# Sums, differences and weight splits placed on VectorE alone, in a two-layer diffusion backbone

## The chip, the core and the metric

The kernel runs on one NeuronCore of a Trainium2 chip. TensorE (PE in the profile, with its weight loads as PEld) multiplies, VectorE (DVE), ScalarE (ACT) and GpSimd (POOL) work on tiles in SBUF, SyncE (SP) issues the DMAs that bring the weights from HBM. TensorE writes to PSUM, which has 8 banks of 128 partitions x 512 floats. Each engine works through its own instructions in order; semaphores hold an instruction until what it needs is done. The metric is the time on the device in microseconds, the median of three runs.

## The reference

All data is float32. There are 512 latent tokens and 256 context tokens with 1024 features, and two layers. Cut to what matters:

```
for l in range(2):
    ml, mc = ada(c, ada_w[l], ada_b[l]), ada(c_ctx, ada_w[l], ada_b[l])     # 9 vectors of 1024 each
    h += 0.5 * m[2] * swiglu(modulate(h, norm_ffn1, m[0], m[1]), ffn1_w_gu, ffn1_w_down)
    n  = modulate(h, norm_mix, m[3], m[4])
    h += m[5] * concat(retention(n @ w_in), fourier(..), attention(..), spatial_gate(..)) @ w_out
    h += 0.5 * m[8] * swiglu(modulate(h, norm_ffn2, m[6], m[7]), ffn2_w_gu, ffn2_w_down)
out = rms_norm(h_lat)
# swiglu(h) = (silu(a) * b) @ w_down, with a, b = split(h @ w_gu); w_gu 1024 x 5632, w_down 2816 x 1024
```

In the second layer the context is needed only up to the keys and values of the mixing; its second feed-forward block then runs on the 512 latent tokens.

## The kernel before

**Numbers in two parts.** TensorE multiplies float32 data in a rounded format (fp32r). To keep accuracy each operand is split: ScalarE casts it (`hi`), and a subtraction makes the rest, `lo = x - hi`. A product is three matmuls: hi hi, hi lo, lo hi (`mm3`). So every piece of weights, 128x512, needs a cast on ScalarE and a subtraction (`w_subs`), and so does every tile of activations (`split_t`). A *split* below is that subtraction.

**Fewer products.** Most of the three first feed-forward blocks is multiplied by quarters in a scheme with 7 products in place of 8 (Strassen's, in a form with sums T1 to T4 of activation quarters and in-place sums of weight quarters). The sums of weight quarters are made by GpSimd in place in the raw weight tiles (`w_sums`, `raw<-raw`); those of activations by `t_task` and `hid_sums`.

**A feed-forward block** takes its 22 columns of 128 hidden features in segments of 4 (the first of 2 or 6). For each segment: two `pair`s (7 products x 2 weight pieces, each piece 12 matmuls of 128x384), giving hidden tiles; then the *down stage*, `down_fast`, again 7 products x 2 pieces:

```
for no, nm, bank, start, end, to in ((1, "11", "b", ...), (5, "T1", "c", ...), (6, "T2", "b", ...),
                                     (3, "22", "c", ...), (7, "T3", "b", ...), (2, "21", "a", ...), (4, "T4", "b", ...)):
    for dh in range(2):
        w = yield from self.getp(("dw", l, which, f, no, dh))
```

After every half piece (6 matmuls, one bank) VectorE adds the bank, times the gate, into the residual H (`upd`, `H<-b,modG,H`): a tile of 384 tokens in one instruction, or, where it crosses from latent to context tokens, a 128 and a 256 one, here called an update pair. A down stage has 28 such half pieces: 4 of 384, 16 pairs, 8 of 384.

**Weights** come as raw tiles of 512 KB (4 buffers), are cut in 2 to 4 pieces, and up to 8 pieces (`NP`) are held ready or in use. A raw tile is given back, and the next one loaded, when its last piece is split.

**The order of the instructions** is made by a planner in the program itself: tasks are generators with priorities, and a clock for each engine (`Eng`: a fixed cost and a rate, for VectorE 68 ns and 0.96 elements/ns, for GpSimd 100 ns and 0.42) says when it would be free. The planner decides when a task emits its next instruction, and twice it decides on which engine: `any2` (a sum, difference or product of two SBUF tiles goes to whichever of VectorE and GpSimd would end first), and `w_subs` (a weight split goes to GpSimd when it is at least `FAR` = 3 pieces ahead of TensorE, VectorE's clock is ahead of the planner's time and GpSimd's is not). Its clocks know nothing of engines getting in each other's way. In the profile all instructions that go through `Eng` have line 127; TensorE's have lines 242 to 283.

Of the kernel before, what the change touches and what calls it, by code (L numbers as in the profile page):

```python
# [35 lines left out]
def f32v(ap):  # L36
    return ap.bitcast(F32)


def _free(ap):  # L40
    n = 1
    for x in ap.shape[1:]:
        n *= x
    return n
# [94 lines left out]


class Kernel:
    FAR, SB, NS = 3, 130.0, 3
    RP = 2
    TG, BM = 300.0, 4000.0
    NM, NK = 3, 0
# [72 lines left out]

    def any2(self, op, out, a, b):

        n = _free(out)
        if any(x.tensor.name == self.psn for x in (a, b)):
            return self.V(op, out, a, b)
        v = max(self.V.t, self.t) + self.V.fixed + n / self.V.rate
        g = max(self.G.t, self.t) + self.G.fixed + n / self.G.rate
        return (self.V if v <= g else self.G)(op, out, a, b)


    def pe(self, cols, rows, floor, reads, out):
# [213 lines left out]
    def w_subs(self):  # L443
        for j, (key, r, view, dep, free) in enumerate(self.pieces):
            yield (lambda: j in self.wh)
            w, hi, src = self.wh.pop(j)
            far = (lambda: j - self.pnext >= self.FAR and self.G.t <= self.t)
            yield (lambda: (self.force > j or self.V.t <= self.t + self.slack(j, self.SWV) or far()) and self.T.ready(hi) <= self.t + 200.0)
            lo = w[:, 1]
            if len(src.shape) == 3:  # L450
                lo = lo.rearrange("p (a b) -> p a b", a=src.shape[1])
            (self.G if far() and self.V.t > self.t else self.V)("tensor_sub", lo, src, f32v(hi))
            self.wt[j] = w
            self.pcv = j + 1
            if free:
                self.dead(self.rawt.pop(r))
                self.rlive -= 1
                self.w_load()
# [1833 lines left out]
```

## Time and profile before

| | |
|---|---|
| median of 3 runs | 2625.94 us (2621.76 to 2627.26) |
| profiled execution | 2626.68 us, its span 2624.7 us |
| TensorE busy | 2539.7 us, 97%, mean granted clock 0.989 |
| VectorE busy | 2029.7 us, 77% |
| ScalarE busy | 1252.0 us, 48% |
| GpSimd busy | 1318.5 us, 50% |
| HBM read | 247.59 MB, 95 GB/s over the span |

TensorE's matmuls are pipelined, so its busy time is no proof of full speed; where it waits is told better by the chain of waits, which follows the work that ended last back to the start. A row of the timeline may stand for several instructions in a row (xN); its names are those of the first ones' form. Names are `out<-in`: H the residual, b a PSUM bank, w a weight piece, raw a raw weight tile, u and t activations.

### The profile page before, as it was taken

The numbers are of one execution on the slowest core, as the hardware profiler recorded it, in microseconds if no ns is written. First come the engines' busy times: TensorE is split into PE (matmuls) and PEld (weight loads), VectorE is DVE, ScalarE is ACT, GpSimd is POOL, SyncE is SP. The second block draws the span as 40 slices with busy tenths as digits, with TensorE's granted clock in tenths as the row PEclk, the third lists the DMA queues.
The fourth block names the chain that finished last, engine by engine and source line by source line (L and its number), as shares of the span: only waits on it lengthen the run. The fifth ranks groups of instructions, "written<-read, shape, count | busy, mean of one in ns | idle before, by whom it ended". The sixth has DMA issues, their size and how long they took to land.

```text
span 2624.7 us, 44882 instructions
## 1 busy us (share of the span) xinstructions
PE 2539.7 (97%) x17116; PEld 2422.2 (92%) x17116; DVE 2029.7 (77%) x3526; ACT 1252.0 (48%) x2576; POOL 1318.5 (50%) x1080
## 2 busy tenths in 40 slices
PE   7999999999999989999999999999999999899998
PEld 5888999999998978889999989999999888899998
DVE  5766787878679886776787877878878788987776
ACT  4433344455646543333444544444446645544445
POOL 3635656733232354555774547667734331544443
PEclk9999999999999999999999999999999999999999
DMA  8455322222111155553223112222232211133332
GB/s 283 142 187 177 113 73 89 65 83 57 49 57 41 43 173 183 188 169 129 81 65 97 49 42 77 68 72 73 73 91 65 61 57 41 57 101 101 100 103 72
DMA packets 193622, 252.57 MB, mean 96 GB/s; under 512 B 12188, under 2 KB 160896, under 8 KB 193408
## 3 DMA queue, kind: packets, MB, share of 16 engines
q1 hardware_dynamic: 187152, 246.82, 29.6%
q10 hardware_dynamic: 6256, 2.90, 0.4%
q8 instruction: 134, 2.20, 0.4%
q14 instruction: 80, 0.66, 0.1%
HBM read 247.59 MB, written 2.10 MB: 95 GB/s over the span
## 4 chain that ended last, share of the span: by engine, by line
PE 76%; DVE 16%; DMA 2%; issue 2%; ACT 2%; POOL 1%; SPq 0%; ACTq 0%; POOLq 0%; DVEq 0%
PE b L242 47%; PE b L244 25%; DVE u L127 7%; DVE t L127 3%; DVE w L127 3%; PE b L255 2%; PE b L283 2%; DVE H L127 1%; DMA adaraw<-in_ada_w_dram 1%; ACT u L127 1%; ACT w L127 1%; DMA raw<-in_ffn_w_gu_dram 1%; SPq L393 0%; POOL nacc L127 0%; ACT t L127 0%
## 5 line engine op out<-in xcount | busy, mean ns | idle before, releaser
L242 PE MATMUL b<-u,w 128*128 128x384 f32 (+1 forms) x8736 | 1449.1, 326 | 9.9 <-DVE adasum L127 5.4
L242 PEld LDWEIGHTS b<-u,w 128*128 128x128 f32 x8736 | 1429.0, 189 | 28.2 <-issue 15.3
L127 ACT CAST w<-raw 128x512 fp32r<-128x512 f32 x949 | 575.7, 620 | 564.3 <-PE b L242 216.2
L127 DVE TENSOR_TENSOR w<-raw,w 128x512 fp32r<-128x512 f32 x674 | 640.9, 962 | 228.6 <-ACT w L127 220.4
L127 POOL TENSOR_TENSOR raw<-raw 128x512 f32<-128x512 f32 x416 | 616.1, 1502 | 345.1 <-DMA raw<-in_ffn_w_gu_dram 130.0
L127 POOL TENSOR_TENSOR w<-raw,w 128x512 fp32r<-128x512 f32 x275 | 383.6, 1408 | 509.3 <-ACT w L127 468.9
L244 PE MATMUL b<-u,w 128*128 128x256 f32 (+2 forms) x3888 | 582.4, 308 | 15.4 <-ACT u L127 11.5
L244 PEld LDWEIGHTS b<-u,w 128*128 128x128 f32 x3888 | 541.9, 193 | 39.7 <-ACT u L127 13.1
L127 DVE SCALAR_TENSOR_TENSOR H<-b,modG,H 128x128 f32<-128x128 f32 (+3 forms) x832 | 365.1, 474 | 134.6 <-PE b L244 76.6
L244 PE MATMUL b<-w,u 128*128 128x256 f32 x2172 | 281.1, 286 | 1.8 <-DVE w L127 1.8
L244 PEld LDWEIGHTS b<-w,u 128*128 128x128 f32 x2172 | 271.1, 193 | 6.8 <-DVE w L127 2.2
L127 ACT CAST u<-u 128x384 fp32r<-128x384 f32 (+4 forms) x318 | 140.9, 464 | 126.6 <-DVE u L127 83.2
L127 DVE TENSOR_TENSOR u<-u 128x384 fp32r<-128x384 f32 (+8 forms) x226 | 164.2, 746 | 11.5 <-ACT u L127 10.7
L127 POOL TENSOR_TENSOR u<-u 128x384 fp32r<-128x384 f32 (+3 forms) x138 | 119.9, 878 | 95.0 <-ACT u L127 94.5
L127 ACT CAST u<-t 128x384 fp32r<-128x384 f32 (+2 forms) x162 | 74.5, 471 | 185.8 <-DVE t L127 182.2
L127 ACT COPY t<-b 128x384 f32<-128x384 f32 (+5 forms) x223 | 99.6, 448 | 125.0 <-PE b L242 79.3
L127 POOL TENSOR_TENSOR nacc<-nacc,t 128x256 f32<-128x256 f32 (+2 forms) x112 | 89.7, 801 | 123.2 <-ACT t L127 119.1
L127 DVE TENSOR_TENSOR t<-t,b 128x384 f32<-128x384 f32 (+3 forms) x216 | 106.1, 494 | 32.9 <-PE b L242 31.9
L127 DVE TENSOR_TENSOR u<-t,u 128x384 fp32r<-128x384 f32 (+2 forms) x150 | 104.8, 704 | 10.9 <-ACT u L127 9.8
L127 DVE TENSOR_TENSOR u<-u,t 128x384 f32<-128x384 f32 (+1 forms) x108 | 102.6, 958 | 12.6 <-POOL u L127 4.8
L244 PE MATMUL b<-u 128*128 128x256 f32 (+5 forms) x516 | 104.6, 336 | 3.0 <-DVE u L127 2.8
L127 DVE TENSOR_TENSOR u<-b,u 64x256 fp32r<-64x256 f32 (+3 forms) x175 | 91.1, 525 | 20.3 <-ACT u L127 18.4
(99 smaller groups left out, 1556.9 us busy)
## 6 DMA issues: line engine op xcount, KB each, us to landing
raw<-in_ffn_w_gu_dram SPq DMA_DIRECT2D x176, 512.0 KB
adaraw<-in_ada_w_dram SPq DMA_DIRECT2D x114, 512.0 KB
raw<-in_ffn_w_down_dram SPq DMA_DIRECT2D x88, 512.0 KB
raw<-in_w_in_dram SPq DMA_DIRECT2D x28, 512.0 KB
raw<-in_w_out_dram SPq DMA_DIRECT2D x32, 256.0 KB
u<-in_ada_w_dram SPq DMA_DIRECT2D x14, 512.0 KB
u<-in_ada_w_dram SPq DMA_DIRECT2D x16, 384.0 KB
raw<-in_w_in_dram SPq DMA_DIRECT2D x16, 256.0 KB
```

The lines of the kernel that those rows point to most:

```text
L127: getattr(self.eng, name)(*args, **kw)
L242: self.nc.tensor.matmul(out, a, b, start=start, stop=stop, skip_group_check=True)
L244: self.nc.tensor.matmul(out, a, b, start=start, stop=stop)
L255: self.nc.tensor.matmul(out[q:q + 32], self.cs[:, k], x, start=start, stop=stop)
L283: self.nc.tensor.transpose(out, in_, self.ident[:p, :p])
```

## The change

`any2` no longer chooses: every sum, difference or product that goes through it is issued on VectorE. In `w_subs` the third condition and the choice of engine go: a weight split is always VectorE's, issued when the piece is due or when VectorE's clock is near the planner's time. GpSimd keeps the sums of weight quarters, most of the sums for the norms (`nacc`), the power for 1/sqrt and the decay tables. The constant `FAR` goes.

```
-    FAR, SB, NS = 3, 130.0, 3
+    SB, NS = 130.0, 3
...
     def any2(self, op, out, a, b):
-        n = _free(out)
-        if any(x.tensor.name == self.psn for x in (a, b)):
-            return self.V(op, out, a, b)
-        v = max(self.V.t, self.t) + self.V.fixed + n / self.V.rate
-        g = max(self.G.t, self.t) + self.G.fixed + n / self.G.rate
-        return (self.V if v <= g else self.G)(op, out, a, b)
+        return self.V(op, out, a, b)
...
             w, hi, src = self.wh.pop(j)
-            far = (lambda: j - self.pnext >= self.FAR and self.G.t <= self.t)
-            yield (lambda: (self.force > j or self.V.t <= self.t + self.slack(j, self.SWV) or far()) and self.T.ready(hi) <= self.t + 200.0)
+            yield (lambda: (self.force > j or self.V.t <= self.t + self.slack(j, self.SWV)) and self.T.ready(hi) <= self.t + 200.0)
...
-            (self.G if far() and self.V.t > self.t else self.V)("tensor_sub", lo, src, f32v(hi))
+            self.V("tensor_sub", lo, src, f32v(hi))
```

In the programs' order, 453 instructions leave GpSimd for VectorE: 275 weight splits (128x512) and 178 others, mostly splits of 128x384 (59) and 128x256 (53) activations. With VectorE's clock later, the planner also gives 26 additions of the norm's shift to ScalarE that VectorE had.

Where it shows most is the down stage. The rows are those of the third one in the second layer's first block; `w_17262` is the eighth of its 14 pieces, `w_17272` the ninth, `u_17305`/`u_17301` and `u_17340`/`u_17334` hold the sums of hidden tiles for the sixth and seventh product. On GpSimd before:

```order
L127 TENSOR_TENSOR w_17262<-raw_17042,w_17262 128x512
L127 TENSOR_TENSOR w_17272<-raw_17014,w_17272 128x512
L127 TENSOR_TENSOR raw_17042<-raw_17111,raw_17042 128x2x256
L127 TENSOR_TENSOR u_17292<-u_16716,u_17292 128x384
L127 TENSOR_TENSOR u_17305<-u_16981,u_17305 128x384 x2
L127 TENSOR_TENSOR u_17340<-u_16981,u_17340 128x384 x2
L127 TENSOR_TENSOR w_17323<-raw_17042,w_17323 128x512
L127 TENSOR_TENSOR w_17338<-raw_17092,w_17338 128x512
```

and on VectorE before, at the same place, where no weight split stands between the 28 half pieces' updates:

```order
L127 TENSOR_TENSOR u_17292<-u_16716,u_17292 128x384
L127 SCALAR_TENSOR_TENSOR H_91<-b_78,modG_14952,H_91 128x128
L127 SCALAR_TENSOR_TENSOR H_91<-b_78,modG_14952,H_91 128x256
L127 SCALAR_TENSOR_TENSOR H_91<-b_78,modG_14952,H_91 128x128
L127 SCALAR_TENSOR_TENSOR H_91<-b_78,modG_14952,H_91 128x256
L127 SCALAR_TENSOR_TENSOR H_91<-b_78,modG_14952,H_91 128x128
L127 SCALAR_TENSOR_TENSOR H_91<-b_78,modG_14952,H_91 128x256
L127 TENSOR_TENSOR u_16981<-u_16981,t_17030 128x384
```

With the change, VectorE from the last split of activations on:

```order
L127 TENSOR_TENSOR u_17334<-u_16981,u_17334 128x384 x2
L127 SCALAR_TENSOR_TENSOR H_91<-b_78,modG_14949,H_91 128x128
L127 SCALAR_TENSOR_TENSOR H_91<-b_78,modG_14949,H_91 128x256
L127 SCALAR_TENSOR_TENSOR H_91<-b_78,modG_14949,H_91 128x128
L127 SCALAR_TENSOR_TENSOR H_91<-b_78,modG_14949,H_91 128x256
L127 TENSOR_TENSOR w_17262<-raw_17042,w_17262 128x512
L127 SCALAR_TENSOR_TENSOR H_91<-b_78,modG_14949,H_91 128x128
L127 SCALAR_TENSOR_TENSOR H_91<-b_78,modG_14949,H_91 128x256
L127 TENSOR_TENSOR w_17272<-raw_17018,w_17272 128x512
L127 TENSOR_TENSOR w_17332<-raw_17042,w_17332 128x512
```

The split of the eighth piece has moved from GpSimd's list to a place in VectorE's that lies behind the updates of the stage's first 14 half pieces (4 of 384 and 10 pairs, two of the pairs in the rows shown) and behind all its activation splits. Nine further weight splits follow among the later updates. Counted through the program, the same sequence stands in eight of the twelve down stages of this kind: the last two of each block of the first layer, and all four of the second layer's first block.

## Rows read from the trace of the kernel before

**Rows 1.** Page, part 1: busy time, share of the span, instructions.

```profile
PE 2539.7 (97%) x17116; PEld 2422.2 (92%) x17116; DVE 2029.7 (77%) x3526; ACT 1252.0 (48%) x2576; POOL 1318.5 (50%) x1080
```

**Rows 2.** Page, part 4: the chain of waits by engine, share of span.

```profile
PE 76%; DVE 16%; DMA 2%; issue 2%; ACT 2%; POOL 1%; SPq 0%; ACTq 0%; POOLq 0%; DVEq 0%
```

**Rows 3.** Chain of waits, 1537 to 1945 us, by engine, tile, line.

```profile
by line: PE b L242 99.9%; PE b L244 0.1%
```

**Rows 4.** Chain of waits, 560 to 975 us, same columns.

```profile
by line: PE b L244 59.9%; DVE u L127 13.5%; DVE t L127 5.8%; PE b L283 4.8%; DVE w L127 3.7%; issue 2.8%; DVE H L127 2.4%; ACT u L127 2.2%; DMA adaraw<-in_ada_w_dram 1.2%; DVE sm L127 1.0%; ACT t L127 0.7%; ACT w L127 0.5%; POOL u L127 0.4%
```

**Rows 5.** Stretches of the span: length, busy time of each engine, clock.

```profile
core 0: us, PE busy (x) PEld busy (x) DVE busy (x) ACT busy (x) POOL busy (x), PEclk, DMA share, GB/s
...
300.00:560.00 260.00, 260.00 (x1503) 260.00 (x1503) 205.35 (x310) 115.24 (x224) 166.74 (x123) 1.00 0.26 80
...
560.00:975.00 415.00, 400.32 (x2951) 374.13 (x2950) 343.61 (x728) 235.75 (x512) 151.18 (x159) 0.99 0.20 63
...
1222.00:1440.00 218.00, 218.00 (x1264) 218.00 (x1263) 171.85 (x255) 99.57 (x195) 137.39 (x97) 1.00 0.25 76
...
1537.00:1945.00 408.00, 408.00 (x2357) 408.00 (x2357) 322.00 (x477) 183.37 (x359) 264.93 (x190) 1.00 0.25 77
```

**Rows 6.** Groups by line and form: count, busy us, mean ns, idle before.

```profile
L127 DVE TENSOR_TENSOR w<-raw,w 128x512 fp32r<-128x512 f32 x674 | 640.9, 962 | 228.6 <-ACT w L127 220.4 <-PE b L242 0.3
...
L127 POOL TENSOR_TENSOR w<-raw,w 128x512 fp32r<-128x512 f32 x275 | 383.6, 1408 | 509.3 <-ACT w L127 468.9 <-PE b L244 24.6 <-DMA raw<-in_ffn_w_down_dram 14.1
...
L127 POOL TENSOR_TENSOR raw<-raw 128x512 f32<-128x512 f32 x416 | 616.1, 1502 | 345.1 <-DMA raw<-in_ffn_w_gu_dram 130.0 <-DVE w L127 102.9 <-DMA raw<-in_ffn_w_down_dram 56.8
...
L127 POOL TENSOR_TENSOR u<-u 128x384 fp32r<-128x384 f32 x59 | 62.3, 1071 | 24.4 <-ACT u L127 24.4
```

**Rows 7.** VectorE in order of time: start us, length us, instruction, waits.

```profile
1724.28 1.88 DVE L127 TENSOR_TENSOR w<-raw,w 128x512 fp32r<-128x512 f32 x3
...
1746.89 1.03 DVE L127 TENSOR_TENSOR u<-u 128x384 fp32r<-128x384 f32 x2 [0.58 <-ACT u L127]
...
1769.36 1.78 DVE L127 TENSOR_TENSOR w<-raw,w 128x512 fp32r<-128x512 f32 x1
```

**Rows 8.** GpSimd in order of time, before and in one down stage.

```profile
1762.58 1.60 POOL L127 TENSOR_TENSOR w<-raw,w 128x512 fp32r<-128x512 f32 x1
...
1768.98 1.61 POOL L127 TENSOR_TENSOR raw<-raw 128x512 f32<-128x512 f32 x1
...
1773.95 3.01 POOL L127 TENSOR_TENSOR w<-raw,w 128x512 fp32r<-128x512 f32 x2 [3.37 <-ACT w L127]
...
1785.12 8.80 POOL L127 TENSOR_TENSOR w<-raw,w 128x512 fp32r<-128x512 f32 x7
```

**Rows 9.** VectorE in order of time, the same down stage.

```profile
1774.46 0.61 DVE L127 SCALAR_TENSOR_TENSOR H<-b,modG,H 128x384 f32<-128x384 f32 x1
...
1774.99 0.54 DVE L127 TENSOR_TENSOR u<-u,b 128x384 f32<-128x384 f32 x1
...
1775.45 2.31 DVE L127 SCALAR_TENSOR_TENSOR H<-b,modG,H 128x384 f32<-128x384 f32 x5
...
1777.68 0.94 DVE L127 TENSOR_TENSOR u<-u 128x384 fp32r<-128x384 f32 x1
...
1778.55 2.03 DVE L127 SCALAR_TENSOR_TENSOR H<-b,modG,H 128x128 f32<-128x128 f32 x6
...
1781.18 1.83 DVE L127 TENSOR_TENSOR u<-u,t 128x384 f32<-128x384 f32 x2 [0.60 <-POOL u L127]
...
1782.93 7.38 DVE L127 SCALAR_TENSOR_TENSOR H<-b,modG,H 128x128 f32<-128x128 f32 x22
...
1790.61 0.74 DVE L127 SCALAR_TENSOR_TENSOR H<-b,modG,H 128x128 f32<-128x128 f32 x2 [0.30 <-PE b L242]
```

**Rows 10.** VectorE, unbroken updates in the first such down stage.

```profile
395.51 6.58 DVE L127 SCALAR_TENSOR_TENSOR H<-b,modG,H 128x128 f32<-128x128 f32 x20
```

**Rows 11.** VectorE's waits, 1537 to 1945 us: total, times, longest.

```profile
DVE w L127 <- ACT w L127: 49.9, 48, 2.3
```

## Prediction

> **What bounds the kernel now.** I read the busy times first, then the chain of waits, then stretches, then single stages. TensorE is busy 97% of the span, VectorE 77%, GpSimd 50% [rows 1], and the chain is 76% TensorE and 16% VectorE [rows 2]: 0.16 x 2624.7 = 420 us in which something waits for VectorE. These are not spread evenly. From 1537 to 1945 us the chain is TensorE alone [rows 3]. The same holds where TensorE is busy all of a stretch [rows 5]: 300 to 560, 1222 to 1440, 1537 to 1945, together 260 + 218 + 408 = 886 us. These are the feed-forward blocks once the modulation is computed; nothing that VectorE or GpSimd does there costs time now, at the granted clock of 1.00. In the mixing, 560 to 975, TensorE has 60 + 5 of 100 and VectorE most of the rest [rows 4].
>
> So the change can win only outside the 886 us, and can lose everywhere. The first question is whether TensorE still never waits inside them.
>
> **The prices.** Three weight splits in a row with GpSimd idle take 1.88 us, 0.60 each after the first's start-up [rows 7]; the mean over all of VectorE's is 962 ns and GpSimd's mean is 1408 [rows 6]. Beside one of GpSimd's sums, of 1.61 from 1768.98, a split took 1.78 [rows 7, 8]. Two splits of 384 take 1.03, so 0.47 each and 0.08 for the end [rows 7]; on GpSimd one is 1071 ns [rows 6]. An update pair is 7.38 / 11 = 0.67; five updates (three of 384 and a pair) take 2.31, so a 384 one is (2.31 - 0.67 - 0.08) / 3 = 0.52 [rows 9].
>
> **What VectorE gains in work.** 275 weight splits x 0.60 = 165 us, and 178 others at 0.47 or below, at most 84: some 230 us in all. Off go 26 shift additions, a few us, and the time that VectorE's own instructions now lose beside the moved ones. VectorE goes from 2029.7 to some 2200 us, 84% of the span. The average would fit. The down stages do not.
>
> **One down stage, step by step.** A piece is 12 matmuls at 408.00 / 2357 = 0.173 us [rows 5], 2.08 us; a half piece 1.04. At 1790.61 VectorE waits for TensorE again [rows 9], with the 16th pair, which is the update of the 20th half piece (4 of 384 precede the pairs). So the stage began on TensorE at 1790.55 - 20 x 1.04 = 1769.75, and its eighth piece at 1769.75 + 7 x 2.08 = 1784.3. VectorE begins the first update at 1774.46 [rows 9], 3.7 us after that half piece ended at 1770.8: it comes into the stage late, from splits that met GpSimd's sums, and works off the lag until 1790. It can, because GpSimd has the splits: two from 1773.95 (the eighth and ninth piece's) and seven from 1785.12 [rows 8].
>
> With the change VectorE's list from the first update to the eighth piece's split holds 4 updates of 384 (2.08), an addition from PSUM (0.47, since it took 0.54 [rows 9]), 10 pairs (6.70), 8 instructions of 384 on SBUF tiles (3.76; before it was three) and the split (0.60): 13.6 us. From 1774.46 that ends at 1788.1. TensorE wants the piece at 1784.3, so it waits 3.8 us. The wait is not only a lag: the split is queued behind the update of the 14th half piece, which TensorE finishes just as it reaches the eighth piece. Even a VectorE with no lag makes it wait 0.67 + 0.60 = 1.27 us, and again 0.67 + 0.60 - 1.04 = 0.23 at the ninth piece, whose split stands behind the 15th half piece. That is the lower end, 1.5 us.
>
> When VectorE starts the stage is the unknown. Ahead of it one split joins its list (+0.60), and the GpSimd split of 1.60 at 1762.58 [rows 8] goes, which can free VectorE of up to that much waiting, less if it waited for a weight sum instead. Net -1.0 to +0.6; I take -0.4, near the middle. Within the 13.6 us I add no contention: GpSimd's one remaining sum of these tiles needs the eighth split done first. If I am wrong on that, 8 instructions lose 0.94 - 0.55 = 0.39 each (the u<-u at 1777.68 against the first of two free ones) [rows 7, 9] and the split 1.18: 4.3 us more. So a stage costs 3.4 us, with ends at 1.5 and 3.8 + 0.6 + 4.3 = 8.7.
>
> Behind the waiting piece nothing else gets late at first: the nine splits that follow are 0.60 each, with updates of 0.67 or 2 x 0.52 between them, under 2.08 a piece. They give raw tiles back some 12 us later than GpSimd did, so the next block's weights land later; the next pair's first piece is needed only at 1769.75 + 14 x 2.08 = 1798.9 plus the wait, and I cost that at nothing. If it is late too, the stage goes towards its upper end.
>
> Eight stages have this sequence of instructions, and unbroken runs of 20 or 22 updates in the trace show the same saturated VectorE, in the first of them at 395.51 as in the one above [rows 9, 10]. 8 x 3.4 = 27 us. In the other four, TensorE also has the modulation's matmuls in between and waits for their DMAs; I take 0 there (ends 0 and 4 x 1.5 = 6).
>
> **The rest of the span**, 2624.7 - 886 = 1739 us, has VectorE on the chain for 420 of them, 24%. Spread evenly, 230 x 1739 / 2624.7 = 152 us of new work lie there; if a quarter is felt, +37. Against it, a weight split loses (962 - 680) / 962 = 29% of its time beside GpSimd (a free one lasts 1.88 - 2 x 0.60 = 0.68) [rows 6, 7]; of GpSimd's time the moved splits and those of 384 alone are (383.6 + 62.3) / 1318.5, a third [rows 1, 6]. At most 420 x 0.29 x 0.34 = 41 us leave the chain; half of it, since much of VectorE's chain reads PSUM, is 20. GpSimd itself has 1% of the chain [rows 2], 26 us, of which perhaps half goes. +37 - 20 - 13 = +4, which I round to 0, with ends -67 (41 + 26, nothing added) and +37.
>
> **The sum** is made on the profiled execution: 2626.68 (span 2624.7 and 2 us around it) + 27 + 0 = 2653.7; the median of the runs shown is 0.7 lower, so 2653.
>
> **Rivals.**
> *The port is freed and the kernel gets faster.* Mechanism: splits on VectorE wait for GpSimd's at the layer's seams and in the mixing, and with 453 of these gone the chain shortens there by the 41 + 26 us that are the upper end above, less half of the +37. For it: 962 against 680 ns, and the two subtractions at 1781.18 that waited 0.60 for GpSimd's split and then took 1.83, not 1.03 [rows 7, 9]. Against it: GpSimd keeps its 616.1 us of weight sums [rows 6], and TensorE must not wait in the down stages, where the order makes it. With no stall there: 2626 - 67 + 18 = 2577 at best, with the middle value of relief 2626 - 33 + 18 = 2611. It decides if VectorE enters the stages without lag and the seams give more than 12 us. The Trainium skill, page "SBUF — State Buffer", section "Who interferes with whom", speaks for this rival: VectorE and GpSimd share a pair of ports as an exclusive lock, and a VectorE instruction with two SBUF inputs fully blocks against a GpSimd one that reads SBUF. The trace agrees with it: 1.78 us for a split beside a sum, 0.60 without [rows 7, 8].
> *The lead hides it.* Eight piece buffers are 8 x 2.08 = 16.6 us of matmuls, and VectorE's splits often wait for ScalarE's casts, 48 times and 49.9 us from 1537 to 1945 [rows 11]: there the weights are as far ahead as the buffers let them. If such lead carried through the stage, nothing would change: 2626 (2621 to 2631). Against it: the instructions are issued in order, and the split stands behind the update.
> *VectorE becomes the bound.* If sums meet the splits after all, or raw tiles come late, the stage costs its upper end, and other stages start to wait: 2626 + 8 x 8 = 2690.
>
> **Chances.** A stall in the eight stages of 1.5 to 5.5 us with the rest within +-10: 2632 to 2672, 0.70. Port freed and faster: 0.11. Lead hides it: 0.09. VectorE the bound, above 2672: 0.10. What a measurement can tell from no change is about 0.2%, 5 us. So faster 0.11, same 0.10 (the second rival and a little of the forecast's lower edge), slower 0.79. The range must leave out 2 in 10: it reaches from 2622 to 2678.
>
> **What would show it.** In the changed profile: TensorE's waits on VectorE's w, none now from 1537 to 1945, come to about 3.4 us a stage, once per 87 us, and the stretch of 408 grows by 14; VectorE at 84%, GpSimd at 770 us or so; VectorE's mean split nearer 800 ns than 962. It is wrong if the chain from 1537 to 1945 is still TensorE alone, or if the stall sits elsewhere: at the seams, or at the first piece after a down stage.

## The result, and the profile after

The kernel after takes **2640.29 us** (median of 4 runs, 2637.9 to 2642.16) against 2623.85 us of the kernel before on the same chip: a ratio of 1.0059, 95% interval 1.0047 to 1.007. It is slower, by 0.6%. Forecast were 2653 us and a range of 2622 to 2678.

The page of the kernel after, its busy times and the chain by engine, beside [rows 1, 2]:

```profile
PE 2548.8 (97%) x17116; PEld 2430.1 (92%) x17116; DVE 2157.0 (82%) x3954; ACT 1259.1 (48%) x2601; POOL 795.5 (30%) x627
...
PE 74%; DVE 20%; DMA 2%; issue 2%; ACT 1%; POOL 0%; SPq 0%; POOLq 0%; DVEq 0%; ACTq 0%
```

VectorE has 428 instructions more, but only 127 us more busy time, where some 170 were forecast. The chain from 1537 to 1945 us, which was TensorE alone [rows 3], is now (TensorE's lines 242 and 244 are 237 and 239 in the kernel after):

```profile
by line: PE b L237 72.5%; DVE u L127 9.0%; DVE H L127 7.7%; DVE w L127 6.5%; DVE t L127 3.0%; issue 1.0%; ACT w L127 0.3%; DVEq L127 0.0%; ACTq L127 0.0%
```

TensorE's waits from 1530 to 2000 us (total us, times, longest) are one row:

```profile
PE b L237 <- DVE w L127: 15.4, 4, 4.2
```

With two each from 300 to 600 (7.4 us) and 1240 to 1500 (7.4 us) that makes eight waits, 30.2 us, 3.8 us each. The stage of [rows 8, 9] in order of time, TensorE and VectorE, from the first update to the eighth piece:

```profile
1780.64 0.60 DVE L127 SCALAR_TENSOR_TENSOR H<-b,modG,H 128x384 f32<-128x384 f32 x1
...
1786.75 1.01 DVE L127 TENSOR_TENSOR u<-u 128x384 fp32r<-128x384 f32 x2
1787.68 1.01 DVE L127 TENSOR_TENSOR u<-u,t 128x384 f32<-128x384 f32 x2
1788.62 2.68 DVE L127 SCALAR_TENSOR_TENSOR H<-b,modG,H 128x128 f32<-128x128 f32 x8
1791.22 1.01 DVE L127 TENSOR_TENSOR u<-u 128x384 fp32r<-128x384 f32 x2
1792.16 1.37 DVE L127 SCALAR_TENSOR_TENSOR H<-b,modG,H 128x128 f32<-128x128 f32 x4
1793.46 0.67 DVE L127 TENSOR_TENSOR w<-raw,w 128x512 fp32r<-128x512 f32 x1
...
1794.19 21.13 PE L237 MATMUL b<-u,w 128*128 128x384 f32 x105 [3.71 <-DVE w L127]
```

The list was forecast at 13.6 us and took 13.49 (1780.64 to 1794.13). But the stage loses more than its wait. These are stretches around the wait in the same stage (columns as in [rows 5]; in brackets the number of instructions, the number ahead of the DMA share is the granted clock):

```profile
1785.00:1790.40 5.40, 5.40 (x32) 5.15 (x30) 5.40 (x16) 4.42 (x9) 0.00 (x0) 1.00 0.00 0
1790.40:1794.20 3.80, 0.09 (x2) 0.01 (x1) 3.73 (x10) 0.00 (x0) 0.00 (x0) 0.87 0.00 0
...
1796.00:1798.00 2.00, 2.00 (x8) 2.00 (x7) 2.00 (x5) 0.00 (x0) 0.00 (x0) 0.50 0.00 0
1798.00:1800.00 2.00, 2.00 (x8) 2.00 (x7) 0.82 (x4) 0.00 (x0) 0.00 (x0) 0.50 0.73 186
1800.00:1802.00 2.00, 2.00 (x13) 2.00 (x13) 2.00 (x6) 0.62 (x1) 0.00 (x0) 1.00 0.96 335
```

TensorE stands for 3.7 us, and the clock falls from 1.00 to 0.50, the 1.2 GHz level, until about 1800: 6 matmuls begin in 2 us instead of 12 (the counts in the rows take in those that reach over an edge), while the busy time says 2.00 of 2.00. This is one of the two longer falls, 6.8 us from 1793.2; in the other six stages the clock stood at 0.50 for 3.4 us, as in the stage at 1608:

```profile
1608.90:1612.30 3.40, 3.40 (x12) 3.40 (x12) 2.18 (x5) 0.00 (x0) 0.00 (x0) 0.50 0.00 0
1612.30:1615.00 2.70, 2.70 (x18) 2.70 (x17) 2.22 (x7) 0.00 (x0) 0.00 (x0) 1.00 0.78 223
```

If one takes the k-th weight matmul of either trace and follows the difference of their times, the stretches with the eight stages lose 12.3 us (two stages, 390 to 500 us of the kernel before), 11.2 (two, 1250 to 1430) and 23.9 us (four, 1590 to 1940), together **47.3 us, 5.9 a stage**: 3.8 of waiting and 2.1 behind it. The clock accounts for nearly all of these 2.1: behind the eight waits it stood at 0.50 for 31.6 us in all, and half of that, 15.8 us, is 2.0 a stage. All the rest of the span gives **34.0 us** back; 47.3 - 34.0 = 13.3 us, and the spans differ by 13.6.

Where these 34 come from shows best at the seam of the two layers. The kernel before, GpSimd, VectorE and TensorE in order of time:

```profile
1505.84 1.62 POOL L127 TENSOR_TENSOR raw<-raw 128x512 f32<-128x512 f32 x1
1506.22 3.21 DVE L127 TENSOR_TENSOR u<-t,u 128x384 fp32r<-128x384 f32 x2
1507.41 3.17 POOL L127 TENSOR_TENSOR w<-raw,w 128x512 fp32r<-128x512 f32 x2
...
1510.54 4.73 POOL L127 TENSOR_TENSOR raw<-raw 128x512 f32<-128x512 f32 x3
...
1512.47 3.20 DVE L127 TENSOR_TENSOR t<-u 128x384 f32<-128x384 f32 x2
1515.78 0.56 DVE L127 TENSOR_TENSOR u<-u,t 128x384 f32<-128x384 f32 x1
...
1520.62 0.69 PE L244 MATMUL b<-u,w 128*128 128x384 f32 x1 [5.22 <-ACT u L127]
```

Beside GpSimd a sum of 384 takes 1.6 us, and 0.56 as soon as GpSimd stops at 1515.3; TensorE waits 5.22 us for what comes of them. In the kernel after GpSimd stands idle until 1508.5, and TensorE goes through:

```profile
1502.82 28.76 PE L239 MATMUL b<-u,w 128*128 128x384 f32 x165
...
1505.14 0.55 DVE L127 TENSOR_TENSOR u<-u 128x384 f32<-128x384 f32 x1
1505.61 0.55 DVE L127 TENSOR_TENSOR u<-t,u 128x384 fp32r<-128x384 f32 x1
1506.08 1.01 DVE L127 TENSOR_TENSOR t<-u 128x384 f32<-128x384 f32 x2
```

This seam gives 9.5 of the 34 us back; the others are spread over the span and were not traced one by one. Sums of this kind over the whole span, and the splits [rows 6], in the kernel after:

```profile
L127 DVE TENSOR_TENSOR w<-raw,w 128x512 fp32r<-128x512 f32 x949 | 848.5, 909 | 196.2 <-ACT w L127 186.8 <-PE b L237 2.2
...
L127 DVE TENSOR_TENSOR u<-u 128x384 fp32r<-128x384 f32 x152 | 78.0, 547 | 3.1 <-ACT u L127 3.1
```

The 93 of the kernel before took 655 ns each. The splits' mean fell only from 962 to 909: matched in time with GpSimd's instructions, 605 of the 949 ran alone at 685 ns, but 155 lay wholly beside one at 1439. The Trainium skill, page "SBUF — State Buffer", section "Who interferes with whom", has VectorE and GpSimd contend for a shared port pair, an exclusive lock, when the VectorE instruction reads two SBUF tiles and the GpSimd one reads SBUF, and not when the VectorE instruction reads one. The trace agrees, down to the sums with an operand in PSUM (t<-t,b of 384): in the kernel before they took 551 ns alone and 548 wholly beside a GpSimd instruction.

### The profile page after: what moved, and what is told of

The parts are those of the page before. It is cut to its first block, busy times and chain, and to the rows that moved or that the text cites. A ratio compares the mean times of both kernels' runs of the same rounds, so it can differ in the third digit from the quotient of the medians.

```text
span 2638.3 us, 44737 instructions
## 1 busy us (share of the span) xinstructions
PE 2548.8 (97%) x17116; PEld 2430.1 (92%) x17116; DVE 2157.0 (82%) x3954; ACT 1259.1 (48%) x2601; POOL 795.5 (30%) x627
## 4 chain that ended last, share of the span: by engine, by line
PE 74%; DVE 20%; DMA 2%; issue 2%; ACT 1%; POOL 0%; SPq 0%; POOLq 0%; DVEq 0%; ACTq 0%
PE b L237 42%; PE b L239 29%; DVE u L127 8%; DVE w L127 5%; DVE H L127 4%; DVE t L127 3%; PE b L250 2%; PE b L278 2%; DMA adaraw<-in_ada_w_dram 2%; ACT u L127 1%; ACT w L127 0%; DMA u<-in_x_dram 0%; DVE sm L127 0%; DMA raw<-in_ffn_w_down_dram 0%; DMA raw<-in_ffn_w_gu_dram 0%
## 5 line engine op out<-in xcount | busy, mean ns | idle before, releaser
L237 PE MATMUL b<-u,w 128*128 128x384 f32 (+1 forms) x8736 | 1465.2, 328 | 38.0 <-DVE w L127 31.8
L127 DVE TENSOR_TENSOR w<-raw,w 128x512 fp32r<-128x512 f32 x949 | 848.5, 909 | 196.2 <-ACT w L127 186.8
L127 POOL TENSOR_TENSOR raw<-raw 128x512 f32<-128x512 f32 x416 | 629.5, 1533 | 1110.6 <-DMA raw<-in_ffn_w_gu_dram 657.9
L127 DVE TENSOR_TENSOR u<-u 128x384 fp32r<-128x384 f32 (+7 forms) x364 | 191.2, 549 | 6.8 <-ACT u L127 5.8
L127 POOL TENSOR_TENSOR nacc<-nacc,t 128x256 f32<-128x256 f32 x102 | 80.9, 793 | 359.3 <-ACT t L127 357.8
L127 POOL TENSOR_TENSOR rs<-mse,mhalf 128x2 f32<-128x2 f32 (+4 forms) x41 | 43.8, 1071 | 231.0 <-DVE mse L127 220.9
L127 DVE TENSOR_TENSOR u<-t,u 128x384 fp32r<-128x384 f32 (+3 forms) x167 | 101.4, 610 | 3.2 <-ACT u L127 2.6
L127 ACT CAST u<-b 64x256 fp32r<-64x256 f32 (+3 forms) x175 | 78.1, 453 | 40.1 <-PE b L278 37.3
L239 PEld LDWEIGHTS b<-u 128*128 128x128 f32 (+1 forms) x516 | 79.1, 183 | 16.3 <-DVE u L127 5.1
```

The lines of the kernel that those rows point to most:

```text
L127: getattr(self.eng, name)(*args, **kw)
L237: self.nc.tensor.matmul(out, a, b, start=start, stop=stop, skip_group_check=True)
L239: self.nc.tensor.matmul(out, a, b, start=start, stop=stop)
```

## The experiments

The times are medians; "stages" is what the eight down stages cost against the kernel before in TensorE's matmuls, and "rest" the remainder up to the last weight matmul, from one trace each. The stretches are those given above; with e2 and e5 some 1.3 and 4 us of "stages" lie in them behind the eight stages. The kernel before, measured beside each group of these runs, had medians of 2624.8 to 2626.1 us, against 2623.85 beside the kernel after; so 2 us between two rows say nothing.

| kernel | us | ratio to before, 95% | stages | rest |
|---|---|---|---|---|
| after (both parts) | 2640.3 | 1.0047 to 1.007 | +47.3 | -34.0 |
| e1 sums alone | 2645.2 | 1.0057 to 1.0085 | +25.1 | -8.3 |
| e2 splits alone | 2631.7 | 1.0009 to 1.0027 | +8.8 | -4.5 |
| e3 after, down splits on GpSimd | 2610.3 | 0.9929 to 0.9955 | +14.7 | -29.5 |
| e4 after, 17 fillers | 2668.0 | 1.0144 to 1.0174 | +71.3 | -30.6 |
| e5 after, lead 2 | 2621.9 | 0.998 to 0.9998 | +16.9 | -26.2 |
| e6 after, lead 4 | **2588.9** | 0.9849 to 0.9876 | +3.8 | -41.6 |
| e7 after, 16 fillers | 2639.5 | 1.004 to 1.0068 | +44.9 | -29.4 |
| e8 before, down splits alone on GpSimd | 2606.9 | 0.992 to 0.9945 | 0.0 | -16.5 |
| e9 after, 30 fillers | 2632.1 | 1.0015 to 1.0035 | +35.5 | -29.7 |
| e10 before, lead 4 | 2627.2 | 0.9997 to 1.0015 | +1.8 | -2.5 |
| e11 after, lead 6 | 2601.8 | 0.9897 to 0.9921 | +7.0 | -35.2 |
| e12 splits alone, lead 4 | 2609.5 | 0.9926 to 0.995 | 0.0 | -14.7 |

**The two parts apart.** e1 is the kernel before with the sums' part of the change:

```
 def any2(self, op, out, a, b):
-    ...
+    return self.V(op, out, a, b)
```

> Half of the change: sums and differences of activations go to VectorE, weight splits keep the choice between VectorE and GpSimd (317 of them stand on GpSimd). Theory: the eight waits of TensorE for a weight split, 47 us in all by the aligned traces, come from the weight splits in VectorE's list, and the 31 us won elsewhere come from the activations' splits that no longer sit on GpSimd. Then there is no TensorE wait in the down stages and the time is 2624 - 31 = about 2593 us (2585 to 2605). Rival: the gain elsewhere comes from the weight splits that leave GpSimd, and the activations' part is worth nothing: 2624 us (2618 to 2630). Second rival: the five activation splits that move into each down stage are enough to make VectorE late: above 2630 us.

It took 2645.2 us; the theory missed by 52, and only the band above 2630 holds it. TensorE's first row of waits, and a sum on VectorE:

```profile
PE b L237 <- DVE H L127: 22.3, 17, 1.6
...
L127 DVE TENSOR_TENSOR u<-u 128x384 fp32r<-128x384 f32 x152 | 129.0, 885 | 8.4 <-ACT u L127 8.4
```

All sums are on VectorE and 317 splits on GpSimd, so they meet: 885 ns a sum against 547 in the kernel after. The updates come late, and TensorE waits for banks, not for splits.

e2 is the other part alone:

```
-            (self.G if far() and self.V.t > self.t else self.V)("tensor_sub", lo, src, f32v(hi))
+            self.V("tensor_sub", lo, src, f32v(hi))
```

> The other half: weight splits all on VectorE, sums and differences of activations still go to whichever engine the planner takes to be first. Theory: the waits in the down stages are all there and little of the gain: 2624 + 47 - 0 to 10 = 2660 to 2671 us. Rival (gain comes from the weight splits): 2624 + 47 - 31 = 2640 us, as the whole change.

2631.7 us: both missed. The eighth piece's split stands behind 10 updates there, not 14 (the planner puts one after every second update once sums go to GpSimd), and the eight waits for it come to 4.9 us, 0.6 each. So the wait of 3.8 us belongs to neither part; it comes of the place that the planner found for the split with both.

e3 is the kernel after, with the splits of the down weights free to go to GpSimd again:

```
+            far = (lambda: key[0] == "dw" and j - self.pnext >= self.FAR and self.G.t <= self.t)
-            self.V("tensor_sub", lo, src, f32v(hi))
+            (self.G if far() and self.V.t > self.t else self.V)("tensor_sub", lo, src, f32v(hi))
```

> The whole change, except that the weight splits of the down stages alone may go to GpSimd when they are three pieces ahead (95 weight splits on GpSimd in place of none, 275 before the change). Theory: the waits of TensorE go, the gain elsewhere stays: 2640 - 47 = 2593 us (2585 to 2605), no wait of TensorE for a weight split longer than 1 us between 1537 and 1945 us. Rival, that the stages wait because VectorE is simply too busy: at least half the waits stay, 2615 us or more.

2610.3 us, better than both kernels, between the bands of theory and rival. The rest keeps its gain (-29.5), the stages lose 14.7 and not 47.3. What remains, in order of time:

```profile
1766.76 5.99 POOL L127 TENSOR_TENSOR w<-raw,w 128x512 fp32r<-128x512 f32 x4 [2.45 <-ACT w L127]
1767.07 2.96 DVE L127 TENSOR_TENSOR u<-u 128x384 fp32r<-128x384 f32 x2
1769.96 3.21 DVE L127 TENSOR_TENSOR u<-u,t 128x384 f32<-128x384 f32 x2
...
1773.97 16.36 PE L237 MATMUL b<-u,w 128*128 128x384 f32 x93 [1.12 <-DVE H L127]
```

Four sums beside four splits of GpSimd take as long as these, one for one, where the kernel after needs 1.01 us for two. From e1 to e3 the other 222 splits go from GpSimd to VectorE, which gains 35 us although VectorE has more to do.

**The place in VectorE's list.** e5 and e6 leave every split on VectorE and let it be written into the list earlier, by two or (e6) four pieces:

```
-            yield (lambda: (self.force > j or self.V.t <= ...
+            yield (lambda: (self.force + 2 > j or self.V.t <= ...
```

> The kernel after, with one edit: a weight split may be written into VectorE's list two pieces earlier than the one TensorE has asked for, so the eighth piece's split stands behind 10 updates instead of 14 in the eight down stages; every split stays on VectorE. Theory (the place in VectorE's list makes the wait, and the clock drop follows from the wait): the eight waits of 3.8 us shrink to some 0.5 us, as where 10 updates stand ahead in the kernel with the weight splits alone (0.5 to 0.9 us), and with them most of the 2.1 us per stage of low clock; 2640 less 8 x 5 = 2600 us (2592 to 2612). First rival (VectorE is simply full in these stages, and a split that comes earlier makes the updates late): the waits turn into waits for the updates' banks, 2630 to 2645. Second rival (it is the engine that counts, not the place): no change, 2636 to 2644.

> As the run before, but four pieces earlier: the eighth piece's split stands behind 6 updates. Theory (place in the list): no wait for a split is left in the eight stages, 2640 less 8 x 5.9 = 2593 us (2585 to 2605). First rival (VectorE is full there): splits ahead of the updates push the updates back, TensorE waits for their banks, 2610 to 2645, slower than with two pieces. Second rival (the engine counts): 2636 to 2644.

e5 has 2621.9 us, between the bands of the theory and the first rival; e6 2588.9, inside it, 1.4% under the kernel before and the best of all. In e5 ten updates stand ahead, and TensorE's row is

```profile
PE b L237 <- DVE w L127: 8.2, 15, 0.9
```

two short waits a stage, as each split comes behind every second update. The granted clock stays at 1.00 through all eight stages; the longest of the waits, 0.95 us, and the next one, 0.48, lie here:

```profile
1775.00:1777.00 2.00, 1.24 (x7) 1.24 (x8) 2.00 (x7) 0.00 (x0) 0.00 (x0) 1.00 0.00 0
1777.00:1779.00 2.00, 1.52 (x9) 1.20 (x8) 2.00 (x6) 0.00 (x0) 0.00 (x0) 1.00 0.00 0
```

In e6 six stand ahead and no wait for a split is left there:

```profile
1537.00:1945.00 408.00, 406.52 (x2416) 405.26 (x2416) 356.35 (x584) 184.43 (x369) 161.84 (x114) 1.00 0.24 75
```

TensorE is busy again, 406.5 of 408 us, where [rows 5] had it at 408.00, with VectorE at 356 us of 408: VectorE is not full, and the engine wasn't the cause. VectorE has the same instructions in another order, but for ten that the planner gives to ScalarE (3944 against 3954); in e5 their number is the same, 3954. e11 takes six pieces:

```
+            yield (lambda: (self.force + 6 > j or self.V.t <= ...
```

> The kernel after with a lead of six pieces instead of four. Theory (no wait for a split is left at four, so more lead brings nothing, and updates stand behind more splits): 2588 to 2600 us. Rival (the layer seams and the other stages still wait for splits): 2575 to 2586.

2601.8 us, just outside the theory's band. TensorE's waits for updates (H on line 237) grow from 1.8 to 4.9 us, as the theory says, and the stages cost 3.2 us more; of the 9.6 us by which the two spans differ the other 6.4 lie in the rest and stay open.

**The clock behind the wait.** e4 gives TensorE 17 unread 128x128 matmuls to run while it would wait, in the unused columns of the bank it has just filled:

```
+                if no == 3 and dh == 1 and (l == 1 or f >= 10):
+                    for _ in range(17):
+                        self.nc.tensor.matmul(ps[:, 384:512], ...)
```

> The whole change, with 17 matmuls of 128x128 that nobody reads put on TensorE in front of the eighth piece of each of the eight down stages, so that TensorE is busy during most of the 3.8 us for which it waits for the split. They write into unused columns of PSUM. Theory: the wait itself costs 3.8 us and the granted clock of 0.50 behind it the other 2.1; with TensorE kept busy the clock stays at 1.00 and the time falls by 8 x 2.1 = 17 us, to 2623 us (2617 to 2630). Rival, that the slow matmuls behind the wait come from late operands: no change, 2640 us, or more if the fillers last longer than the wait.

2668.0 us: the experiment failed. The fillers' rows, waits and busy time:

```profile
PE b L1361 <- DVE H L127: 27.9, 8, 3.8
...
L1361 PE MATMUL b<-u,w 128*128 128x128 f32 x136 | 30.0, 408 | 27.9 <-DVE H L127 27.9
```

The bank is still to be read by the 14th update, so the fillers waited for that and ran behind it: 27.9 + 30.0 us instead of 30.2 us of waits, 27.7 more, as the medians differ (2640.3). In the matched matmuls 24.0 of this lie in the stages. e7 and e9 write to a bank whose last update is several back, 16 and 30 times. They begin a new sum in a bank that holds part of a sum, so the down products are not the reference's; the instructions of the kernel after and their order are kept.

```
+                    for _ in range(16):
+                        self.nc.tensor.matmul(banks["c", 1, 0][:, 384:512], ...)
```

> The kernel after, with 16 unread 128x128 matmuls ahead of the eighth piece in each of the eight down stages, into the unused columns of a bank whose update is several updates back, so that they can run while TensorE would wait for the split. In the first run with fillers they took 0.22 us each (30.0 us for 136), so 16 take 3.5 us of the 3.8 us. Theory (behind each wait some 2.1 us go to the lower clock, because TensorE stood still): the stage loses 3.8 us instead of 5.9, the granted clock stays at 1.00 behind it, 2640 less 17 = 2623 us (2618 to 2630). Rival (the 2.1 us behind the wait are the next splits being late too, not the clock): 2640 us (2636 to 2645). Second rival (the fillers wait for an update all the same and run after it): 2650 to 2668.

> The kernel after with 30 instead of 16 unread 128x128 matmuls ahead of the eighth piece in each of the eight down stages. The 16 ran in 1.90 us at a granted clock of 1.00, a wait of 1.95 us was left, and behind it the clock stood at 0.50 as in the kernel after; 30 take 3.56 us and leave some 0.3 us. Theory (the wait costs 3.8 us itself and 2.1 us more by the clock behind it): clock 1.00 through the stage, the stage loses 3.8 us instead of 5.9; 2640 less 17 = 2623 us (2617 to 2630). Rival (the 2.1 us are not the clock but VectorE, which is behind and makes the next pieces late too): the clock stays at 1.00 and the time at 2636 to 2644, with new waits behind the eighth piece.

e7, stretches of the same stage (fillers, wait, behind it):

```profile
1793.50:1795.40 1.90, 1.90 (x19) 1.90 (x18) 1.90 (x7) 0.00 (x0) 0.00 (x0) 1.00 0.00 0
1795.40:1797.80 2.40, 0.45 (x4) 0.13 (x3) 2.33 (x6) 0.00 (x0) 0.00 (x0) 0.83 0.00 0
...
1800.00:1802.00 2.00, 2.00 (x8) 2.00 (x7) 2.00 (x5) 0.00 (x0) 0.00 (x0) 0.50 0.05 5
```

The fillers took 0.12 us each at a granted clock of 1.00, not the 0.22 of e4 (which ran at 0.50), so half the wait was left, 1.95 us here, and the clock fell behind it all the same, until 1803.8: 2639.5 us, no gain, by a course that none of the three had. It fell in six of the eight stages, behind waits of 1.77 to 2.68 us; in the other two, behind 2.26 and 2.62, it stayed at 1.00, so here the length of the wait alone doesn't tell whether it falls. One of these two (wait, behind it):

```profile
1703.80:1706.10 2.30, 0.04 (x2) 0.01 (x1) 2.24 (x6) 0.00 (x0) 0.00 (x0) 1.00 0.00 0
1706.10:1710.00 3.90, 3.86 (x21) 3.54 (x22) 2.90 (x8) 0.00 (x0) 0.00 (x0) 1.00 0.07 11
```

e9:

```profile
1786.40:1789.70 3.30, 3.30 (x32) 3.30 (x31) 3.30 (x11) 0.00 (x0) 0.00 (x0) 1.00 0.00 0
1789.70:1790.70 1.00, 0.60 (x4) 0.28 (x3) 0.96 (x2) 0.00 (x0) 0.00 (x0) 1.00 0.00 0
1790.70:1793.00 2.30, 2.29 (x12) 2.06 (x12) 1.26 (x4) 0.00 (x0) 0.00 (x0) 1.00 0.00 0
```

No fall, in this stage or in the seven others, with waits of 0.2 to 1.15 us left. VectorE's list takes as long as before (13.50 us), but the stages lose 35.5 us instead of 47.3. The clock behind the wait is worth (47.3 - 35.5) / 8 = 1.5 us a stage by this; the matched matmuls of the kernel after gave 2.1, its rows at 0.50 2.0. Of e9's 4.4 us a stage, 3.5 are fillers and 0.4 wait; 0.5 stay open. The time, 2632.1, misses the theory's band by 2 us and lies 8.2 below the kernel after, less than the 11.8, since the rest gave 4.3 us less back in this trace.

**What GpSimd's share costs.** e8 and e10 edit the kernel before: the condition of e3, and the lead of e6.

```
-            far = (lambda: j - self.pnext >= self.FAR and self.G.t <= self.t)
+            far = (lambda: key[0] == "dw" and j - self.pnext >= self.FAR and self.G.t <= self.t)
```

> The kernel before, with one edit: of the weight splits only those of the down weights may go to GpSimd; the sums go to either engine as before. Theory (GpSimd's splits outside the down stages lengthen VectorE's instructions there, 685 ns alone and 1.2 to 1.4 us beside GpSimd, more than they save): as between the two kernels that send all sums to VectorE (2645 and 2610), some 20 to 35 us are won: 2598 us (2590 to 2612). Rival (with sums on both engines the balance evens this out): 2618 to 2630. Second rival (in the down stages GpSimd's sums and splits meet and the waits come back): above 2630.

```
-            yield (lambda: (self.force > j or self.V.t <= ... or far()) and ...
+            yield (lambda: (self.force + 4 > j or self.V.t <= ... or far()) and ...
```

> The kernel before (sums and splits on either engine) with the one edit that took the kernel after to 2589 us: a split may stand four pieces ahead in VectorE's list. It tells whether the lead is worth something by itself or only where it takes the change's waits away. Theory (the change costs waits in eight stages and gives back some 31 us elsewhere, since VectorE's instructions run shorter with GpSimd quiet; the lead only takes the waits away, of which the kernel before has none): 2618 to 2628 us. Rival (the lead shortens other waits too, and the change is worth little): 2590 to 2610.

e8 took 2606.9 us, e10 2627.2; both theories hold. Splits on GpSimd outside the down stages cost more than they save, and the lead on the kernel before is worth nothing that can be measured. e12 is e2 with e6's line, `self.force + 4 > j`:

> The weight splits all on VectorE with a lead of four pieces, the sums on either engine as before. With the kernel after and the same lead (2589 us) it prices the sums' part of the change where no split is late. Theory (139 sums on GpSimd lengthen VectorE's instructions beside them: its splits take 685 ns alone and 1.2 to 1.4 us beside GpSimd, and GpSimd's own sums of 0.87 us end later than VectorE's 0.55): 2600 to 2615 us. Rival (a sum on GpSimd leaves VectorE room, and its waits are hidden): 2580 to 2592.

2609.5 us, as the theory says. With the lead, then, the kernel before has 2627.2, the splits' part brings it to 2609.5 and the sums' part to 2588.9: some 18 and 21 us, 38 in all. Without the lead the same change costs 16. With each of these edits the planner also writes the instructions in another order; how much of the 18 and 21 us comes of that, and how much of shorter instructions on VectorE, these runs don't separate.

## Why the prediction was right, and where it was not

- **The wait in the down stages: right.** Eight stages, the place, the list of 13.6 us (13.49), one wait for the eighth piece's split. e5 and e6 show the cause: with the splits on the same engine but earlier in its list the wait shrinks to 0.95 us at most and is then gone.
- **Its length: 3.4 forecast, 3.8 measured.** The term that failed is the -0.4 for an earlier start of VectorE. With the matmuls matched, its first update came 4.89 us into TensorE's stage and 4.51 before; over the eight stages it is 0.5 us later in the mean. The free GpSimd bought VectorE no earlier start. This error of 0.8 is partly made up by smaller ones: TensorE's stage before began at 1769.96, not 1769.75, its seven pieces take 14.72 us, not 14.56, and the list was 0.1 shorter. That no sum meets GpSimd inside the list was right; GpSimd stood idle 30.24 us ahead of its next weight sum:

```profile
1808.14 1.45 POOL L127 TENSOR_TENSOR raw<-raw 128x512 f32<-128x512 f32 x1 [30.24 <-DMA raw<-in_ffn_w_gu_dram]
```

- **What follows the wait: the step "behind the waiting piece nothing else gets late" held for pieces, and missed the clock.** It took the granted clock of 1.00 as given, but behind each of the eight waits it stood at 0.50. A stage costs 5.9 us, not 3.4; 47.3 in all instead of 27. e9 shows that it is the standing still, with 1.5 us a stage; e7, that waits of about 2 us still did it in six of eight stages; behind e5's waits, 0.95 us at most, it stayed at 1.00.
- **The rest of the span: 0 forecast, -34 measured.** The step that the runs speak against is the +37 for new work. It spread 230 us evenly over VectorE's share of the chain, as if VectorE's work were a sum of fixed prices; from e1 to e3 VectorE got 222 splits more and the rest gave 21 us more back. The relief alone, -20 - 13 = -33, fits the measured -34, but no run takes it apart from the new work, so that its size was right is not shown. At the seam a row of sums went from 1.6 to 0.55 us each, and a wait of 5.22 us went.
- **The total** was 13 us too high because two errors met, 20 us too little in the stages and 34 too much in the rest; that it came so near is partly luck. That its sign was right rests on the stages alone.
- **The rival "the port is freed"** had a chance of 0.11. Its mechanism is there, and its 33 us fit the rest; it fell to the stages, as said there. Without the stall it gave 2577 to 2611, and e6, without the stall, has 2588.9. "The lead hides it" was wrong with the order as it is. "VectorE becomes the bound" was wrong: 82%, and e6 has the same share.
- VectorE's share was forecast a little high (84%, measured 82%) and GpSimd's time a little low (770 us, measured 795.5): its 416 weight sums, longer now at 1533 ns against 1502 [rows 6], make 13 of the 25 us. The mean split (nearer 800 ns forecast, 909 measured) was off because GpSimd's weight sums still meet the splits, 155 of them wholly.

## What to carry to other kernels

When work moves to an engine with an in-order list, ask first what stands ahead of the one instruction that TensorE waits for: here six updates instead of fourteen turned +0.6% into -1.4% with all but ten instructions on the same engines. Price a wait of TensorE with what the clock does behind it; here 3.8 us of waiting cost 5.9. And where two engines get in each other's way, an instruction moved from one to the other takes time off its neighbours too, so a sum of fixed prices is too high.

## What the runs showed of the hardware

- A VectorE instruction on two SBUF tiles takes about two to three times as long beside a GpSimd one: splits 685 ns alone and 1439, sums of 384 0.55 and 1.6 us at the seam. With one operand in PSUM it takes the same, 551 ns alone and 548.
- Behind waits of TensorE of 3.6 to 4.2 us (kernel after, eight times) the granted clock stood at 0.50, for 3.4 us in six stages and 6.8 us in two, although TensorE was fed again. Behind waits of 1.8 to 2.7 us (e7) it fell in six of eight stages. Behind waits of at most 1.6 us in the down stages of e1, e5 and e9 it stayed at 1.00.
- A clock of 0.50 doesn't show in the busy time: 2.00 of 2.00 us with 6 matmuls begun as with 12.
- Matmuls of 128x128 took 0.12 us each at a clock of 1.00 (16 in 1.90 us), 0.22 in the stages of e4, at 0.50.
